# A hybrid decoder step on one NeuronCore: attention values by head and a later normalisation, tiles zeroed once, and a tail in which decays move to ScalarE and loads to GpSimd's queue

## The chip, the cores and the metric

The kernel runs on one core of one Trainium2 chip. The metric is the time of one execution on the device, in microseconds. The core has five engines that run their own instruction streams in order and wait for one another by semaphores: TensorE (PE in the profile; PEld is its weight load), VectorE (DVE), ScalarE (ACT), GpSimd (POOL) and SyncE (SP). SP, ACT and POOL also issue DMAs.

## The reference, cut to what matters

One inference step of a decoder layer: 1024 prompt tokens and 32 sampled ones (8 sequences of 4), model width 1024, four head groups of width 512 that share one input and one output projection.

```python
# x <- LayerNorm(alpha * x + W_out [y_A | y_B | y_C | y_D])
# A: gated DeltaNet, 4 heads of 128, chunks of 64, solved in its triangular form
#    S_t = exp(g_t) S_{t-1} + beta_t k_t (v_t - exp(g_t) S_{t-1}^T k_t)^T,  o_t = S_t^T q_t
# B: Mamba-2 SSD, 8 heads of 64, 2 groups of B/C, state 64; gated by SiLU, then
#    y / rms(y) * w_norm
# C: FoX: softmax(q k^T + sum of log-forget gates, causal) v, 8 heads of 64, times a SiLU gate
# D: cross attention, 4 heads of 128, into 256 memory tokens
```

The step also attends the sampled tokens to 4096 cached ones per sequence, and returns the new caches and states.

## The kernel before

**Stages.** The trace falls into four stretches. From 0 to about 755 us the input projections run, mixed with the attention of the sampled tokens over the cached pages. From 755 to 1157 us FoX runs, woven with the DeltaNet solve and scan and with the rest of the projections. From 1157 to 1420 us is the tail: the output projection, mixed with the eight SSD chunks and the sampled tokens' last steps. The rest is the LayerNorm of the last token tile and its stores. All large products are in float32, split into a high and a low part where the projections need it.

**What sets the order.** The Python code issues steps of several generators in turn (`weave((fox, 64), (gdn, 37))`). A scheduler in the framework then reorders the instructions of each engine by its own planned times, and tile pools set the waits: a tile with `bufs=1` can be loaded again only when the last reader of its former content is done. A queue is never reordered on the chip: what stands behind a waiting instruction waits too.

**FoX** (`fox`). Four pairs of heads, one after the other. A pair loads `vt` (its values for all 1024 tokens, 512 KB, from the DRAM tensor `vD`, one buffer) and the gate `g2` on SP's queue, and q, k and the cumulative gates on GpSimd's. `with behind(self.gl, ...)` orders the SP loads behind a DeltaNet gate load. For each head: scores in PSUM tile `fs`, minimum and exponential on VectorE and ScalarE (`S`), transposes (`ft`) copied to `P`, products `fo<-P,vt` (L620), and VectorE multiplies `fo` into `g2`. After both heads the sums of the exponentials are inverted, spread over 64 columns (`rr`), transposed (`fr`), and multiplied into `g2` (L640).

**DeltaNet** (`gdn`). Eight units (four heads in two halves). `gdn_solve` inverts triangular blocks: it reads `A` (loaded on SP from the DRAM tensors `aD..A`, `big("A")`) and `D1`, whose diagonal 16x16 blocks come from the DRAM tensor `dX` by eight DMAs on SP (L1041) after VectorE has zeroed the tile (L1039). `gdn_scan` then carries the state over the chunks (`su` matmuls) and loads `qd`, `Kt`, `QK` and its gate `g2` (L1051).

**SSD** (`ssd`). Each of eight chunks loads `E` (printed as `bE`), `bx` and a gate on SP. GpSimd copies the C rows of `bx` into a zero-padded tile `Cz` (L1355), so that one matmul (`bb`) makes both groups' products. VectorE takes the difference of cumulative decays for each of 8 heads (L1378), ScalarE the exponential, GpSimd multiplies by `cb` (L1382). The result `y` goes, times the norm weight, to the DRAM tensor `mixD[1]`.

**Output projection** (`out`, `mixed`, `out_w`). 16 row blocks of `w_out` in four groups of four (12 to 15, 8 to 11, 0 to 3, then 4 to 7, SSD's group). For each group and each of eight token tiles `mixed` loads the mixer tile `mr` (256 KB, on SP), ScalarE makes the high part `mh`, GpSimd the rest `ml` (L1546), and 24 matmuls `op` of 128x512 follow (L1574). The tiles have two buffers. In the last group the sampled tokens' tile (8) stands first; its matmul reads `accs`, which VectorE adds up in `out_s` (L1535); after each tile comes its LayerNorm (`lr` and `acc` on GpSimd).

## Time and profile before

| | us |
|---|---|
| timed runs | 1434.15, 1447.03, 1447.47 (median 1447.03) |
| the profiled execution | 1434.86 |
| its span in the trace | 1433.1 |
| PE busy in the span | 1329.7 (93%) |
| DVE, ACT, POOL busy | 823.8, 494.7, 442.4 |

The span is what the trace covers; the profiled execution's own time is 1.8 us longer. In a row of the trace the number in brackets is the time for which the engine stood idle just before the instruction, and behind the arrow is what ended that idle time. Digits at the end of names are left out, so that `g` stands for the `g2` tiles and `D` for `D1`.

### The profile page before, as it was taken

The numbers are of one execution on the slowest core, as the hardware profiler recorded it, in microseconds if no ns is written. First come the engines' busy times: TensorE is split into PE (matmuls) and PEld (weight loads), VectorE is DVE, ScalarE is ACT, GpSimd is POOL, SyncE is SP. The second block draws the span as 40 slices with busy tenths as digits, with TensorE's granted clock in tenths as the row PEclk, the third lists the DMA queues.
The fourth block names the chain that finished last, engine by engine and source line by source line (L and its number), as shares of the span: only waits on it lengthen the run. The fifth ranks groups of instructions, "written<-read, shape, count | busy, mean of one in ns | idle before, by whom it ended". The sixth has DMA issues, their size and how long they took to land. (4 is left out here: it accounts for less than half of the span.)

```text
span 1433.1 us, 30270 instructions
## 1 busy us (share of the span) xinstructions
PE 1329.7 (93%) x11222; PEld 1110.0 (77%) x11222; DVE 823.8 (57%) x2141; ACT 494.7 (35%) x1280; POOL 442.4 (31%) x465
## 2 busy tenths in 40 slices
PE   7999999999899999999998899898988979999995
PEld 6899888888778877888887878776766756666764
DVE  4523223256576767534245655677676648856588
ACT  4422222233435343322233244454444421213232
POOL 1445322233425444432212100011111026544456
PEclk9999999999999999999999999899999999999998
DMA  6559888978778897888877834657547576655322
GB/s 246 196 169 374 331 299 323 321 269 281 240 284 306 282 307 248 303 287 323 308 259 175 239 91 118 239 147 208 137 129 252 175 234 205 198 160 121 96 67 106
DMA packets 184477, 324.30 MB, mean 226 GB/s; under 512 B 47177, under 2 KB 110954, under 8 KB 184330
## 3 DMA queue, kind: packets, MB, share of 16 engines
q1 hardware_dynamic: 113744, 241.39, 50.4%
q10 hardware_dynamic: 41930, 59.11, 11.6%
q0 software_dynamic: 28656, 21.88, 6.2%
q8 instruction: 88, 1.44, 0.4%
q14 instruction: 59, 0.48, 0.1%
HBM read 262.23 MB, written 60.01 MB: 225 GB/s over the span
## 5 line engine op out<-in xcount | busy, mean ns | idle before, releaser
L356 PE MATMUL pj<-xh,wh 128*128 128x352 f32 x1152 | 382.2, 333 | 13.1 <-ACT wh L341 5.0
L356 PE MATMUL pj<-xh,wl 128*128 128x352 f32 x1152 | 379.5, 329 | 3.3 <-DVE wl L342 3.3
L356 PE MATMUL pj<-xl,wh 128*128 128x352 f32 x1152 | 379.1, 329 | 0.0
L356 PEld LDWEIGHTS pj<-xh,wh 128*128 128x128 f32 x1152 | 219.1, 191 | 28.1 <-issue 10.7
L356 PEld LDWEIGHTS pj<-xh,wl 128*128 128x128 f32 x1152 | 219.8, 191 | 11.5 <-issue 6.3
L356 PEld LDWEIGHTS pj<-xl,wh 128*128 128x128 f32 x1152 | 219.3, 190 | 10.6 <-issue 9.9
L1574 PE MATMUL op<-wo,mh 128*128 128x512 f32 x512 | 162.9, 398 | 3.1 <-DVE lr L1587 1.6
L672 POOL DMA_INDIRECT lf<-in_logf,ix x64 | 67.9, 1062 | 203.4 <-DVE cb L675 163.4
L342 POOL TENSOR_TENSOR wl<-wr,wh 128x1024 fp32r<-128x1024 f32 x41 | 97.9, 2387 | 104.3 <-ACT wh L341 94.3
L742 DVE SCALAR_TENSOR_TENSOR Oacc<-Oacc,dmb,dO 128x512 f32<-128x512 f32 x64 | 47.5, 743 | 142.3 <-PE dO L737 134.1
L1574 PEld LDWEIGHTS op<-wo,mh 128*128 128x128 f32 x512 | 95.6, 190 | 29.6 <-issue 6.0
L1574 PE MATMUL op<-wo,ml 128*128 128x512 f32 x256 | 102.0, 401 | 5.5 <-POOL ml L1546 5.5
L917 DVE SCALAR_TENSOR_TENSOR y<-u,cw,y 128x1080 f32<-128x1080 f32 x54 | 80.1, 1484 | 21.9 <-ACT y L915 21.5
L718 PEld LDWEIGHTS dA<-pg,QD 128*32 128x32 f32 x2048 | 59.8, 109 | 39.7 <-issue 25.8
L718 PE MATMUL dA<-pg,QD 128*32 128x128 f32 x2048 | 80.6, 275 | 7.6 <-DMA pg<-in_cache 7.5
L598 ACT ACTIVATE S<-S,mn 128x512 f32<-128x512 f32 (+2 forms) x96 | 58.5, 610 | 50.8 <-DVE mn L592 24.3
L737 PE MATMUL dO<-pg,dP 128*32 128x512 f32 x512 | 71.8, 605 | 4.1 <-ACT dP L734 3.9
L726 ACT ACTIVATE dmb<-dmb 128x1 f32<-128x1 f32 x64 | 18.7, 293 | 131.6 <-DVE dmb L725 116.3
L1574 PEld LDWEIGHTS op<-wo,ml 128*128 128x128 f32 x256 | 48.4, 189 | 20.2 <-POOL ml L1546 7.1
L592 DVE CUSTOM_DVE_ANT_0 S<-fs,cB 128x512 f32<-128x512 f32 (+2 forms) x96 | 52.5, 551 | 19.9 <-PE ft L219 15.0
L1193 POOL TENSOR_TENSOR rb<-ra,constG 128x4 f32<-128x4 f32 (+1 forms) x9 | 8.7, 971 | 156.5 <-DVE ra L1192 156.5
L620 PE MATMUL fo<-P,vt 128*64 128x128 f32 x576 | 47.9, 288 | 9.6 <-DMA vt<-vD 7.7
(521 smaller groups left out, 2450.2 us busy)
## 6 DMA issues: line engine op xcount, KB each, us to landing
pg<-in_cache SPq DMA_DIRECT2D x256, 512.0 KB
wr<-in_w_in SPq DMA_DIRECT2D x48, 512.0 KB
k<-kD POOLq DMA_DIRECT2D x16, 512.0 KB, 18.2
wq<-in_w_out SPq DMA_DIRECT2D x16, 512.0 KB
mr<-mixD SPq DMA_DIRECT2D x32, 256.0 KB
xr<-in_xT SPq DMA_DIRECT2D x8, 528.0 KB
gateD<-gt ACTq DMA_DIRECT2D x24, 176.0 KB
mrow<-in_w_mem SPq DMA_DIRECT2D x8, 512.0 KB
```

What stands on the lines that cost most here:

```text
L342: (eng or self.se).tensor_tensor(out=l, in0=r, in1=h.bitcast(F32), op=ALU.subtract)
L356: nc.tensor.matmul(ps[:n], lhsT=w[:, k, :], rhs=x[:, k, s], start=(k == 0 and q == 0), stop=(k == KD - 1 and q == 2))
L592: nc.vector.tensor_tensor_reduce(out=S[:, :w], in0=p[:, :w], in1=cB[:, c0:c1], op0=ALU.add, op1=ALU.min, scale=1.0, scalar=3e38, accum_out ...
L598: nc.scalar.activation(out=S[:, :w], in_=S[:, :w], func=AF.Exp, scale=-1.0, bias=mn[:, 0:1], accum_out=rs[:, qt, h2, i:i + 1])
L620: d = nc.tensor.matmul(o[64 * half:64 * half + 64, 0:128], lhsT=vt[:, kt, 64 * h2:64 * h2 + 64], rhs=P[qt, b4], start=(kt == 0), stop=(kt ...
L672: nc.gpsimd.indirect_dma_start(out=lf, out_offset=None, in_=I["logf"], in_offset=bass.IndirectOffsetOnAxis(ap=ix[:, j:j + 1].bitcast(U32), ...
L718: nc.tensor.matmul(ps[32 * b:32 * b + 32, 0:n], lhsT=QD[:, 4 * gr + b, hp, :], rhs=key(hp, b), start=(hp == 0), stop=(hp == 3), tile_posit ...
L726: nc.scalar.activation(out=mb[:, 1:2], in_=m, func=AF.Exp, scale=-1.0, bias=mb[:, 0:1])
L737: nc.tensor.matmul(po[32 * b:32 * b + 32, :], lhsT=P[:n, 32 * b:32 * b + 32], rhs=value(b), start=True, stop=True, tile_position=(0, 32 * b))
L742: nc.vector.scalar_tensor_tensor(out=O_, in0=O_, scalar=mb[:, 1:2], in1=po, op0=ALU.mult, op1=ALU.add)
L917: nc.vector.scalar_tensor_tensor(out=y, in0=u[:, i:i + CWD], scalar=w[:, i:i + 1], in1=y, op0=ALU.mult, op1=ALU.add)
L1574: nc.tensor.matmul(p[:m], lhsT=l[:, k, :], rhs=W[k][0][:, w, s], start=(k == 0 and q == 0), stop=(k == kn - 1 and q == 2))
```

## The change

FoX: `vt` is held by head (256 KB) with two buffers, and the load of each head is issued at the head's start; the projection writes `vD` in that layout. The normalisation becomes a generator, `fox_norm`, that runs in two steps within the next pair's work, and for the last pair at the end. DeltaNet: two lasting tiles `D1z` are zeroed once by GpSimd in place of a `D1` zeroed by VectorE for each unit; the second content of `D1` gets a tile of its own. SSD: `Cz` and its copies go; two matmuls over 64 rows each, into two PSUM tiles, make the products. The eight differences of a chunk go from VectorE to ScalarE (Relu, then Exp with scale -1). The multiplication by the norm weight goes from `y` into `w_out`'s rows 4 to 7. Output: the weights of the next group are loaded one group ahead into a second pool, mixer tiles have three buffers and are loaded by GpSimd's queue (all but the first two), and the last group takes the sampled tokens' tile second.

```diff
 def fox_v(self, hp):
+        vv = vt[:, :T].rearrange("p (h n c) -> p n h c", h=2, c=64)
-            self.copy(vt[:, 512 * a:512 * a + 512], p)
+            self.copy(vv[:, 4 * a:4 * a + 4], p.rearrange("p (n h c) -> p n h c", h=2, c=64))
-    def fox(self, hp):
+    def fox(self, hp, ended):
-        vt = fx.tile([128, 8, 128], F32, tag="vt", name="vt", bufs=1)
...
-            if h2 == 0:
-                with behind(self.gl, hd - GL):
-                    nc.sync.dma_start(vt, self.vD[hp].rearrange("p (n c) -> p n c", c=128))
+            vt = fx.tile([128, 8, 64], F32, tag="vt", name="vt", bufs=2)
+            with behind(self.gl, hd - GL):
+                nc.sync.dma_start(vt, self.vD[hp][:, 512 * h2:512 * h2 + 512].rearrange("p (n c) -> p n c", c=64))
+                if h2 == 0:
                     nc.sync.dma_start(g2, self.gateD[8 + hp])
...
+                next(ended, None)
                 o = self.g("fo")
...
+        return self.fox_norm(hp, g2, rs)
+
+    def fox_norm(self, hp, g2, rs):
         ri = fx.tile([128, 8, 2], F32, tag="ri", name="ri", bufs=2)
...
+            if a == 1:
+                nc.scalar.dma_start(self.mixD[2][:, hp, :], g2)
+            yield
 def gdn(self):
+        self.D1z = [self.ga.tile([128, 4, 32], F32, name=f"D1z{i}") for i in range(2)]
+        for t in self.D1z:
+            nc.gpsimd.memset(t, 0.0)
 def gdn_inv(self, i):
-        D1 = self.ga.tile([128, N, 32], F32, tag="D1", name="D1", bufs=2)
-        nc.vector.memset(D1, 0.0)
+        D1 = self.D1z[i % 2]
 def ssd(self):
-            for g in range(2):
-                nc.gpsimd.tensor_copy(cz[G[g], g, :], bx[G[g], 5, :])
...
-            nc.tensor.matmul(p[:, 128:384], lhsT=bx[:, 4, :], rhs=cz, start=True, stop=True)
+            p2 = self.g("bb")
+            for g, o in enumerate((p[:, 128:256], p2[:, 0:128])):
+                nc.tensor.matmul(o, lhsT=bx[G[g], 4, :], rhs=bx[G[g], 5, :], start=True, stop=True)
...
             for hh in range(8):
-                nc.vector.tensor_scalar(out=E[:, hh, :], in0=E[:, hh, :], scalar1=self.gam[:, n, 4 + hh:5 + hh], scalar2=0.0,
-                                        op0=ALU.subtract, op1=ALU.min)
-            nc.scalar.activation(out=E, in_=E, func=AF.Exp)
+                nc.scalar.activation(out=E[:, hh, :], in_=E[:, hh, :], func=AF.Relu, scale=-1.0, bias=self.gam[:, n, 4 + hh:5 + hh])
+            nc.scalar.activation(out=E, in_=E, func=AF.Exp, scale=-1.0)
...
-            nc.vector.tensor_tensor(out=y, in0=y, in1=_bc(self.pv[:, 91:95], 128), op=ALU.mult)
 def out_w(self, k0, k1, pool=None):
+            if k0 == 4:
+                f = self.pv[:, 87 + k:88 + k]
+                nc.scalar.activation(out=w[:, 0, :], in_=r, func=AF.Identity, scale=f)
+                nc.vector.scalar_tensor_tensor(out=w[:, 1, :], in0=r, scalar=f, in1=w[:, 0, :].bitcast(F32), op0=ALU.mult, op1=ALU.subtract)
 def mixed(self, k0, k1, n):
-        raw, mh, ml = (self.ow.tile([128, kn, 128], d, tag=t, name=t, bufs=2) ...
-        nc.sync.dma_start(raw, self.mixD[k0 // 4][:, q0:q0 + kn, n * 128:(n + 1) * 128])
+        pool, nb, eng = self.mixp                    # (ow, 2, nc.sync) at first, then (op, 3, nc.gpsimd)
+        raw, mh, ml = (pool.tile([128, kn, 128], d, tag=t, name=t, bufs=nb) ...
+        eng.dma_start(raw, self.mixD[k0 // 4][:, q0:q0 + kn, n * 128:(n + 1) * 128])
 def out(...):
-        for n in ((8,) if last else ()) + tuple(range(8)):
+        for n in (0, 8, 1, 2, 3, 4, 5, 6, 7) if last else range(8):
 the calls in the tail, with KO = (8, 0):
+                V = self.out_w(KO[0], KO[0] + 4, ow2)
                 run(self.out(12, 16, W, first=True, pre=pre))
-                for k in KO:
-                    W = self.out_w(k, k + 4)
-                    self.out_s(k, W)
-                    run(self.out(k, k + 4, W))
+                self.out_s(KO[0], V)
+                W = self.out_w(KO[1], KO[1] + 4)
+                run(self.out(KO[0], KO[0] + 4, V))
```

TensorE's instructions stand in the same order in both programs up to the one that runs at about 755 us in the trace of before, so the first of the four stretches is the same.

On SP's queue, at the load of the third pair's values (`vt<-vD_81`) in the program before (`g_12226` is the DeltaNet's second gate tile, `D_12851` a `D1` tile, `dq` and `g_15416` belong to cross attention):

```order
L1057 DMA Kp<-aD2Kp 128x512
L809 DMA dq<-dqD_86 128x1024
L1051 DMA g_12226<-gateD_125 128x512
L568 DMA vt<-vD_81 128x1024
L1041 DMA D_12851<-dX_122 16x4x16 x5
L1057 DMA A<-aD2A 128x512
L1041 DMA D_12851<-dX_122 16x4x16 x3
```

The same place in the changed program, where one pair has two such loads:

```order
L1064 DMA g_12226<-gateD_125 128x512
L570 DMA vt<-vD_81 128x512
L1054 DMA D1z_11226<-dX_122 16x4x16 x8
L1070 DMA A<-aD2A 128x512
L819 DMA dq<-dqD_86 128x1024
L1070 DMA Vp<-aD2Vp 128x512
L1070 DMA Kp<-aD2Kp 128x512
L1070 DMA Kt<-aD2Kt 128x512
L1070 DMA qd<-aD2qd 128x512
L1070 DMA QK<-aD2QK 128x512
L821 DMA g_15420<-gateD_134 128x1024
L1064 DMA g_12620<-gateD_126 128x512
```

The pair's first load still stands behind the DeltaNet's gate; a DeltaNet unit's loads and the next gate, `g_12620`, stand between it and the second head's, which follows two rows later. Counted in `fo` matmuls on TensorE's queue (288 in all), the eight DeltaNet units' last steps stand behind 72, 108, 137, 161, 190, 216, 245 and 281 of them before, and behind 39, 72, 101, 129, 154, 183, 216 and 245 now.

On TensorE, at the end of FoX's second pair in the program before (`fr` is the normalisation, `cT` cross attention, `lp`, `lt` and `su` DeltaNet):

```order
L620 MATMUL fo<-P,vt 64x128 x7
L219 MATMUL fr<-constG,rr 128x128 x4
L219 MATMUL cT<-constG,P 128x128 x3
L588 MATMUL fs<-k_13209,q_13208 128x512
L589 MATMUL fs<-k_13210,q_13208 128x512
L591 LDWEIGHTS identb
L591 MATMUL fs<-foxm,identb 128x128
L1092 MATMUL lt<-P_12482,D_12089 32x16 x16
L1164 MATMUL su<-u,Kt 128x128
L1165 MATMUL su<-u,QK 128x128
L1167 MATMUL su<-S,qd 128x128
L219 MATMUL fr<-constG,rr 128x128 x4
```

And the end of a pair in the changed program:

```order
L624 MATMUL fo<-P,vt 64x128 x7
L219 MATMUL fr<-constG,rr 128x128 x4
L591 MATMUL fs<-k_13187,q_13186 128x512
L592 MATMUL fs<-k_13188,q_13186 128x512
L1173 MATMUL su<-S,wkT 128x128
L1119 MATMUL lp<-DT_12845,A 32x32 x8
L219 MATMUL cT<-constG,P 128x128 x4
L219 MATMUL ft<-constG,S 128x128 x3
```

The second `fr` now follows three `fo` later, with the next pair's work and more of the DeltaNet's between the two.

On GpSimd's queue, around one SSD chunk in the program before (`hst` and `Cg` belong to the chunk ahead, `rsB`, `xtl` and `bE` follow):

```order
L1405 TENSOR_TENSOR hst<-hst,hcd 128x256
L1376 TENSOR_TENSOR Cg<-Cg,bx 128x512
L1355 COPY Cz_16195<-bx 64x128 x2
L1546 TENSOR_TENSOR ml<-mr,mh 128x512 x2
L1416 TENSOR_TENSOR rsB<-bso,constG 128x1
L1362 TENSOR_TENSOR xtl<-xdt,etl 128x512
L1382 TENSOR_TENSOR bE<-bE,cb 128x512 x2
L1546 TENSOR_TENSOR ml<-mr,mh 128x512
```

And in the changed program:

```order
L1414 TENSOR_TENSOR hst<-hst,hcd 128x256
L1386 TENSOR_TENSOR Cg<-Cg,bx 128x512
L1560 TENSOR_TENSOR ml<-mr,mh 128x512
L1558 DMA mr<-mixD_136 128x4x128
L1560 TENSOR_TENSOR ml<-mr,mh 128x512
L1558 DMA mr<-mixD_136 128x4x128
L1425 TENSOR_TENSOR rsB<-bso,constG 128x1
L1369 TENSOR_TENSOR xtl<-xdt,etl 128x512
L1391 TENSOR_TENSOR bE<-bE,cb 128x512
L1560 TENSOR_TENSOR ml<-mr,mh 128x512
L1391 TENSOR_TENSOR bE<-bE,cb 128x512
L1558 DMA mr<-mixD_136 128x4x128
```

The copies `Cz`, ahead of two `ml`, are gone, and each `ml` has a load beside it. In the last group seven of the eight loads stand ahead of the first LayerNorm step on this queue.

## Rows read from the trace of the kernel before

**Rows 1.** Stretches: length; busy (xcount) of PE, PEld, DVE, ACT, POOL; PEclk, DMA, GB/s.

```profile
0.00:755.00 755.00, 720.13 (x6247) 634.16 (x6248) 370.29 (x937) 253.53 (x661) 259.90 (x274) 0.99 0.81 283
755.00:1157.00 402.00, 363.05 (x3567) 295.73 (x3569) 264.08 (x819) 173.26 (x516) 46.52 (x66) 0.95 0.59 175
1157.00:1420.00 263.00, 246.18 (x1414) 180.06 (x1406) 180.15 (x373) 66.42 (x101) 130.01 (x120) 0.99 0.50 147
1141.00:1157.00 16.00, 11.99 (x127) 8.73 (x131) 11.91 (x47) 5.44 (x17) 2.75 (x7) 1.00 0.59 200
```

**Rows 2.** PE's order of time, FoX stage: start, us, instruction, [idle before <-releaser].

```profile
1004.17 0.69 PE L620 MATMUL fo<-P,vt 128*64 128x128 f32 x4 [7.71 <-DMA vt<-vD]
...
1089.90 0.47 PE L219 MATMUL fr<-constG,rr 128*128 128x128 f32 x1 [5.02 <-DVE g L640]
```

**Rows 3.** The stretches just behind three stalls; PEclk is the granted clock.

```profile
1004.00:1009.00 5.00, 4.83 (x18) 3.98 (x19) 2.14 (x5) 0.44 (x2) 0.00 (x0) 0.50 0.00 0
1090.00:1095.00 5.00, 5.00 (x23) 4.71 (x24) 4.67 (x13) 2.62 (x6) 2.48 (x3) 0.53 1.00 365
1303.00:1307.00 4.00, 4.00 (x11) 3.19 (x12) 0.00 (x0) 0.00 (x0) 4.00 (x5) 0.59 0.44 131
```

**Rows 4.** SP's queue in order of time, third pair's loads.

```profile
992.60 0.32 SPq L1051 DMA_DIRECT2D g<-gateD  x1
993.01 0.41 SPq L568 DMA_DIRECT2D vt<-vD  x1
```

**Rows 5.** DVE in order of time, two units of DeltaNet.

```profile
898.51 0.28 DVE L1082 TENSOR_TENSOR AL<-A,constG 32x128 f32<-32x128 f32 x1 [7.40 <-DMA A<-aD1A]
...
1086.25 0.28 DVE L1082 TENSOR_TENSOR AL<-A,constG 32x128 f32<-32x128 f32 x1 [4.07 <-DMA A<-aD3A]
```

**Rows 6.** What SP's queue waited for: total us, times, longest.

```profile
SPq L1041 <- DVE D L1039: 45.9, 4, 16.5
```

**Rows 7.** PE's order of time, tail.

```profile
1246.69 0.50 PE L1574 MATMUL op<-wo,ml 128*128 128x512 f32 x1 [1.81 <-POOL ml L1546]
...
1277.90 0.50 PE L1574 MATMUL op<-wo,ml 128*128 128x512 f32 x1 [0.95 <-POOL ml L1546]
...
1302.81 0.77 PE L1574 MATMUL op<-wo,ml 128*128 128x512 f32 x1 [2.78 <-POOL ml L1546]
...
1372.12 0.62 PE L1576 MATMUL op<-accs,constG 128*32 128x512 f32 x1 [2.79 <-DVE accs L1535]
```

**Rows 8.** POOL in order of time, one SSD chunk's start in the tail.

```profile
1300.78 0.63 POOL L1355 COPY Cz<-bx 64x128 f32<-64x128 f32 x2 [9.18 <-DMA bx<-bD]
1301.49 1.26 POOL L1546 TENSOR_TENSOR ml<-mr,mh 128x512 fp32r<-128x512 f32 x1
```

**Rows 9.** Groups by line and shape from 1157 us, xcount | busy, mean.

```profile
L1546 POOL TENSOR_TENSOR ml<-mr,mh 128x512 fp32r<-128x512 f32 x30 | 40.7, 1358 | 41.1 <-ACT mh L1545 40.6
L1602 POOL TENSOR_TENSOR acc<-acc,lb 128x512 f32<-128x512 f32 x14 | 19.4, 1392 | 10.8 <-DVE acc L1601 5.6 <-DVE lr L1587 5.2
L1378 DVE TENSOR_SCALAR bE<-bE,gam 128x128 f32<-128x128 f32 x64 | 18.1, 344 | 10.2 <-DMA bE<-gS 5.4 <-ACT Cg L1375 4.9
L1588 POOL TENSOR_TENSOR lr<-lr,constG 128x1 f32<-128x1 f32 x8 | 4.8, 601 | 0.0
L1545 ACT CAST mh<-mr 128x512 fp32r<-128x512 f32 x30 | 18.5, 617 | 75.0 <-PE op L1574 52.2 <-DMA mr<-mixD 12.8 <-issue 5.4
L1367 ACT COPY bt<-bb 128x128 f32<-128x128 f32 x8 | 2.1, 263 | 14.5 <-PE bb L1365 14.5
```

**Rows 10.** The tile op alone in a stretch of the last group.

```profile
1374.00:1418.00 44.00, 42.38 (x184) 34.07 (x184) 11.29 (x16) 0.00 (x0) 1.00 0.25 86
```

**Rows 11.** POOL in order of time: two of its DMA issues.

```profile
767.01 0.59 POOL L1057 DMA_DIRECT2D A<-aD0A  x1 [0.30 <-POOL bs L923]
771.03 0.86 POOL L561 DMA_DIRECT2D q<-qD  x1
```

**Rows 12.** The page's costliest groups: POOL's indirect DMAs.

```profile
L672 POOL DMA_INDIRECT lf<-in_logf,ix x64 | 67.9, 1062 | 203.4 <-DVE cb L675 163.4
```

More of the change, by code (lines that the diff above doesn't have):

```diff
@@ L1079, in gdn_solve @@
             self.gdn_inv(i + 1)
[L1080 removed]
+        nc.vector.transpose(out=fl(DT1), in_=fl(D0))
         for q in Q:
@@ L1339, in ssd @@
             nc.gpsimd.tensor_copy(cd[G[g]], self.cdP[G[g], :, 4 + 4 * g:8 + 4 * g])
-        Cz = [sb.tile([128, 2, 128], F32, name=f"Cz{i}") for i in range(2)]
-        for c in Cz:
-            nc.gpsimd.memset(c, 0.0)
         gam8 = self.gS.rearrange("(c n) t -> n c t", n=8)
@@ L1693, in foxes @@
             def foxes():
+                ended = iter(())
                 for hp in range(4):
-                    yield from self.fox(hp)
+                    ended = yield from self.fox(hp, ended)
+                run(ended)
             fox, gdn = foxes(), self.gdn()
```

40 lines of the change are left out of this document (22 added, 18 removed).

## The prediction

> **What bounds the kernel now.** I read the stretches first. Up to 755 us TensorE is busy for 720 of 755 us, from there to 1157 us for 363 of 402, and in the tail for 246 of 263 [rows 1]. No other engine comes near: in the tail GpSimd has 130 us and VectorE 180 of 263, in FoX's stretch VectorE has 264 of 402 [rows 1]. So TensorE bounds every stretch, and a change is worth what it takes out of TensorE's idle time, 39 us in FoX's stretch and 17 us in the tail, plus what the clock loses behind a stall. The reader is to look at TensorE's order of time next, at the instruction that ended each long stall, and then on the engine named there, at what it had waited for.
>
> In FoX's stretch two stalls stand out that the change touches: 7.71 us at 1004.17, ended by the DMA that brought a pair's values, and 5.02 us at 1089.90, ended by VectorE's `g` in the normalisation [rows 2]. In the tail I take four: 1.81, 0.95 and 2.78 us ended by GpSimd's `ml`, and 2.79 us ended by `accs` [rows 7]. Behind three of these TensorE ran for 4 to 5 us at a granted clock of 0.50, 0.53 and 0.59 [rows 3], that is at or near the lower of its two levels, 1.2 GHz, though it was busy all the time. Taken against full clock this costs 5 x 0.50 = 2.5, 5 x 0.47 = 2.3 and 4 x 0.41 = 1.6 us. Shorter stalls get no such term.
>
> **The values by head.** In the program before, the pair's 512 KB go out at 993.01, directly behind a DeltaNet gate load at 992.60 on SP [rows 4], and TensorE stands until 1004.17. In the changed program there are two buffers of one head each, so the next pair's first load needs only the former pair's first head to be done, half a pair earlier, and half the bytes. The gate load still stands ahead of it on the queue, and would hold it as before if the DeltaNet were as late as before; but the DeltaNet's last steps stand 29 to 36 `fo` matmuls earlier, about half a pair of 72. So I take the whole stall: -7.7 - 2.5 = **-10.2**. What is late next at that place is the minimum and the exponential, which both programs have there.
>
> **The normalisation within the next pair.** The stall of 5.02 us is one of a chain: the second `fr` needs VectorE's product with the first, and VectorE stood for 4.07 us until `A` of the DeltaNet had come, at 1086.25, 3.7 us before TensorE went on [rows 5]. Moving `fr` behind three `fo` of the next pair gives TensorE work between the two, but VectorE still stops when `A` is late, and everything that TensorE does there passes VectorE. Bounds: 0, if the wait ends elsewhere, and -5.0 - 2.3 = -7.3. I take **-3**, nearer to nothing, because VectorE's wait is not touched by this part.
>
> **The tiles zeroed once.** SP waited 45.9 us in four waits, once 16.5 us, to start the loads into `D1` until VectorE had zeroed it [rows 6], and `A` is queued behind these loads. The eight zeroings go, and SP then waits only for the last reader of the tile two units before. That makes `A` earlier; VectorE's waits for it were 7.40 and 4.07 us [rows 5], which reach TensorE in part. Bounds 0 and -4.1 (the second whole); I take **-2**.
>
> **The DeltaNet's earlier end.** The order moves the DeltaNet ahead, and its last unit ends behind 245 of 288 `fo`, before behind 281. The last 43 `fo` then run with less to fill TensorE's gaps. A measure of such a stretch is the last 16 us of the stage before, with TensorE busy for 11.99, or idle for 25% [rows 1], against 10% in the whole stretch. 43 of 288 is 15% of 402 us, 60 us, of which about half is FoX's own work (an estimate): 30 us x 15% = 4.5. Bounds 0, if the cross attention fills it, and 9 with all 60 us; I take **+4**. This is the price of the first part: the same shift that frees the gate load takes filler from the end. FoX's stretch together: -10.2 - 3 - 2 + 4 = **-11**.
>
> **The copies in the tail.** All three `ml` stalls have one cause, seen on GpSimd: the copy into `Cz` of the next chunk waits 9.18 us for the DMA that brings `bx`, and the `ml` that TensorE needs stands right behind it in the queue [rows 8]. With the copies gone the `ml` stand behind `Cg`, which reads the chunk's own data. -1.81 - 0.95 - 2.78 - 1.6 = **-7.1**. The products move to two matmuls of half the columns, so TensorE's work stays. The first instruction on GpSimd that now needs the new `bx` is `xtl`; ahead of it stand one or two `ml` more, so that I expect its wait to hide. Bounds 0 to -7.1 belong to a rival below.
>
> **The last group's order.** The sampled tokens' matmul stands second, so `accs` has a token tile's time more, 24 x 44 / 184 = 5.7 us at the last group's pace [rows 10], against 2.79 us of stall: **-2.8**.
>
> **Loads on GpSimd's queue.** 30 loads take GpSimd's own time. Nearby issues of plain DMAs took 0.59 and 0.86 us there [rows 11], an indirect one 1.06 [rows 12]: 30 x 0.59 to 1.06 = 18 to 32 us on an engine that has 133 us to spare in the tail. In the last group GpSimd has per token tile `ml` 1.36, `lr` 0.60 and twice `acc` 1.39, 4.7 us [rows 9], and TensorE needs 5.7 us, so 1.0 us is left, a little more than a plain issue. But seven of the eight loads stand ahead of the first LayerNorm step, with three buffers behind them. Bounds 0 and 7 x 1.06 = +7.4, if they all delay the chain; I take **+1**. A gain I exclude: none of the stalls in [rows 7] was ended by such a load.
>
> **What I cost at nothing.** The eight differences per chunk take 0.344 us each off VectorE [rows 9]. On ScalarE the nearest row of that size is the copy of 128x128 at 0.263 us [rows 9]: 64 x 0.26 = 17 us on an engine busy for 66 of 263. They come ahead of an `mh` of 0.62 us [rows 9] by 8 x 0.26 = 2.1 us at most, covered by a token tile's 5.7 us of matmuls; without that cover 8 chunks x 2.1 = 17 us. The norm weight in `w_out`, the earlier weights and the four buffers for sampled states take away waits that ended no stall of [rows 7]. The drain behind the last matmul keeps its order.
>
> **The sum.** FoX -11.2; tail -7.1 - 2.8 + 1 = -8.9; together -20.1, which makes 1434.9 - 20.1 = 1414.8 against the profiled execution. The median of the three runs is 1447.0, 12.2 us above it, and two of three runs lie there, so at the median's level the same sum gives 1426.9. I predict **1420**, between the two. With all ends at their best: -10.2 - 7.3 - 4.1 - 7.1 - 2.8 = -31.5, 1403. At their worst: -10.2 + 9 - 7.1 - 2.8 + 7.4 = -3.7, 1431 at the profiled level and 1443 at the median's.
>
> **Rivals.**
> First, the stalls in FoX only move: VectorE stops for `A` as before, the values come in time but the next pair's first `fo` waits for VectorE instead, and the end of the stretch has no filler. For it speaks that the stretch has VectorE busy for 264 of 402 us and that its waits are untouched by two of three parts; against it, that the longest stall was a plain transfer. FoX's stretch then gives 0, the tail -8.9: 1426 against 1434.9, within 1%.
> Second, slower: the mixer tiles come late because their loads stand in GpSimd's queue. A load is issued three tiles ahead at best, two tiles of cover are 11.5 us; less `mh` and `ml`, 2.0 us together, 9.5 us are left for a wait on the queue, the issue and the transfer. A wait as that of `Cz`, 9.18 us [rows 8], now on `xtl`, uses this up, and from there each tile behind a chunk is late. Price: at each of 8 chunks the stall at 1302.81 with its clock, 2.78 + 1.6 = 4.4, so +35; with FoX at -11 and `accs` at -2.8 the sum is 1456. For it: `xtl` needs the same transfer, and loads stand behind it in every chunk. Against: it stands later in the chunk than `Cz` did.
> The nearest rows for an issue are 0.59 to 1.06 us while VectorE was at work too. The Trainium skill, SBUF — State Buffer, section "SBUF: two separate sides", speaks against this part: it says that GpSimd cannot write the descriptors of its own DMAs while VectorE runs an operation in a two-port mode, and gives about 620 ns alone and 3100 ns then. By it 30 x 3.1 = 93 us, an estimate from that page, would fill most of GpSimd's idle time in the tail; no row here shows an issue that long.
> Third, the change doesn't do what it says: the values still come behind a late gate load, since that load stands ahead of them on SP in both programs, and GpSimd's wait for `bx` moves to `xtl` with the `ml` behind it. Then only `accs` is gained: 1432.
>
> **Chances.** The forecast 0.58: the causes of the two largest terms are each seen on the engine that waited. The first rival 0.22, the third 0.10, the second 0.10. A measurement of this kernel can tell about 1%, 14 us, from no change. The forecast lies beyond that, the first and the third rival within it, the second on the other side: faster 0.58, same 0.32, slower 0.10. The range takes the forecast's ends at both levels, **1403 to 1443**; the first rival lies in it (1426, at the median's level 1438), the third at the profiled level; what is left out is the second and part of the third.
>
> **What would show it.** In the changed kernel's trace the stall ended by `vt` should be gone and none over 3 us stand ahead of a pair's first `fo`; SP's wait for VectorE's zeroing should be gone and VectorE's waits for `A` shorter; `ml` should end no stall over 1 us behind a chunk's start, and GpSimd's loads should take 0.5 to 1.1 us each. From the first pair's end to the last `fo` the stretch should be some 11 us shorter, the tail some 9. I am wrong if TensorE's idle time near the last pair grows by more than 9 us, or if GpSimd waits at `xtl` as it did at `Cz`.

## The result, and the profile after

The changed kernel takes 1480.39 us (median of 4 runs) against 1442.28 for the kernel before, measured beside it; the ratio is 1.0273, with a 95% interval of 1.021 to 1.0336. I had forecast 1420 with a range up to 1443. The profiled execution has a span of 1476.5 us against 1433.1.

The windows of the changed kernel, cut at the last `dO` of the decode, the last `fr` of FoX and the last `op` (columns as in [rows 1]):

```profile
770.80:1185.60 414.80, 355.81 (x3398) 290.16 (x3391) 250.56 (x787) 166.42 (x500) 47.07 (x63) 0.93 0.59 165
1185.60:1461.60 276.00, 261.66 (x1439) 189.24 (x1437) 162.99 (x304) 85.46 (x165) 142.38 (x130) 0.94 0.45 139
1461.60:1476.50 14.90, 0.40 (x2) 0.00 (x0) 10.82 (x18) 1.72 (x3) 6.51 (x6) 0.67 0.28 106
```

The same cuts in the kernel before (770.0, 1155.6, 1419.9):

```profile
770.00:1155.60 385.60, 348.88 (x3394) 284.54 (x3387) 254.12 (x792) 167.05 (x500) 45.35 (x62) 0.95 0.60 176
1155.60:1419.90 264.30, 247.48 (x1425) 180.63 (x1424) 181.16 (x377) 66.42 (x101) 129.91 (x120) 0.99 0.50 146
1419.90:1433.10 13.20, 0.42 (x2) 0.00 (x0) 9.34 (x13) 1.52 (x2) 6.04 (x6) 0.59 0.32 119
```

The first 770 us are the same within 0.8 us. FoX's stretch is 414.8 us long against 385.6, +29.2; the tail 276.0 against 264.3, +11.7; the drain 14.9 against 13.2. Each length can be taken apart: TensorE's idle time is the length less its busy time, and the clock's part is the length times one less PEclk (rounded to 0.01 in the row, so to 2 us here). In FoX's stretch idle time went from 36.7 to 59.0 us and the clock's part from 19 to 29; in the tail idle time fell from 16.8 to 14.3 and the clock's part rose from 3 to 17. What is left, TensorE's work at full clock, is the same within 3 us. The clock's part counts a low clock also while TensorE stands, where it costs nothing, so the two overlap a little. So FoX's stretch lost some three quarters by standing (22.3 of 29.2 us) and the rest by the clock behind it, and the whole loss of the tail is clock.

The long stalls of TensorE in the changed kernel's order of time:

```profile
937.27 0.47 PE L219 MATMUL ft<-constG,S 128*128 128x128 f32 x1 [6.26 <-ACT P L214]
...
1077.19 0.58 PE L1177 MATMUL su<-u,Kt 128*128 128x128 f32 x1 [5.78 <-DVE u L1174]
...
1113.64 0.47 PE L219 MATMUL ft<-constG,S 128*128 128x128 f32 x1 [11.96 <-ACT P L214]
...
1201.76 0.48 PE L219 MATMUL bt<-constG,bx 128*128 128x128 f32 x1 [4.01 <-DMA bx<-bD]
...
1287.59 0.33 PE L1398 MATMUL by<-bE,xdt 128*64 128x128 f32 x2 [2.45 <-POOL bE L1391]
...
1295.59 0.80 PE L1588 MATMUL op<-wo,mh 128*128 128x512 f32 x1 [3.22 <-ACT wo L1529]
...
1310.99 0.48 PE L1398 MATMUL by<-bE,xdt 128*64 128x128 f32 x2 [3.16 <-POOL bE L1391]
```

None of the stalls of [rows 2] and [rows 7] is there: no `fo` waits for `vt`, no `op` for `ml`, and `accs` ends none. Others stand in their place, longer ones. In the tail one is a wait of TensorE itself for `bx`, the load that `Cz` had waited for before [rows 8]. What had the engines named in FoX's stretch waited for? The rows of ScalarE, VectorE and SP behind the stalls at 937, 1077 and 1113 us:

```profile
936.36 0.34 ACTq L1190 DMA_DIRECT2D out_pgs<-S  x1
936.74 0.48 ACT L214 COPY P<-ft 128x384 f32<-128x384 f32 x1 [6.69 <-DMA mk<-mkD]
...
1074.45 0.28 DVE L1095 TENSOR_TENSOR AL<-A,constG 32x128 f32<-32x128 f32 x1 [7.38 <-DMA A<-aD3A]
...
1097.94 0.60 SPq L1558 DMA_DIRECT2D mr<-mixD  x1
...
1112.36 0.62 ACT L1559 CAST mh<-mr 128x512 fp32r<-128x512 f32 x1 [11.68 <-DMA mr<-mixD]
...
1113.00 0.58 ACT L214 COPY P<-ft 128x512 f32<-128x512 f32 x1
```

At 1113 ScalarE's copy of `P`, which FoX's `fo` needs, stood in its queue behind `mh`, the conversion of the output projection's first mixer tile; its load was issued on SP at 1097.94 and came 14 us later. At 1077 VectorE stood 7.38 us for the `A` of a DeltaNet unit, where the waits of [rows 5] were 7.40 and 4.07 us, and the scan of an earlier unit, which TensorE needed next, stood behind it. At 937 ScalarE stood 6.69 us and copied `P` only when it had issued a store of a DeltaNet state, `out_pgs<-S`. Each time an instruction at the head of an engine's queue waits for a load, or to issue a store, and work of another stage or unit stands behind it.

### The profile page after: what moved, and what is told of

It reads as the page before. It is cut to its first block, busy times and chain, and to the rows that moved or that the text cites. A ratio compares the mean times of both kernels' runs of the same rounds, so it can differ in the third digit from the quotient of the medians.

```text
span 1476.5 us, 30258 instructions
## 1 busy us (share of the span) xinstructions
PE 1348.6 (91%) x11238; PEld 1122.6 (76%) x11238; DVE 806.3 (55%) x2069; ACT 513.5 (35%) x1344; POOL 458.0 (31%) x479
## 3 DMA queue, kind: packets, MB, share of 16 engines
q10 hardware_dynamic: 41930, 59.11, 11.4%
## 5 line engine op out<-in xcount | busy, mean ns | idle before, releaser
L356 PE MATMUL pj<-xh,wh 128*128 128x352 f32 x1152 | 383.2, 333 | 15.4 <-ACT u L214 8.6
L1588 PE MATMUL op<-wo,mh 128*128 128x512 f32 x512 | 168.2, 409 | 3.2 <-ACT wo L1529 3.2
L565 POOL DMA_DIRECT2D k<-kD x16 | 13.2, 828 | 186.8 <-PE fs L594 153.5
L219 PE MATMUL ft<-constG,S 128*128 128x128 f32 x288 | 50.1, 292 | 22.1 <-ACT P L214 19.3
L1560 POOL TENSOR_TENSOR ml<-mr,mh 128x512 fp32r<-128x512 f32 x32 | 43.4, 1358 | 77.9 <-ACT mh L1559 77.8
L736 ACT ACTIVATE dmb<-dmb 128x1 f32<-128x1 f32 x64 | 18.8, 293 | 130.2 <-DVE dmb L735 125.1
```

Of the source, the lines that this page charges most:

```text
L219: self.nc.tensor.transpose(out, in_, self.c("ident", n)[:, :n])
L356: nc.tensor.matmul(ps[:n], lhsT=w[:, k, :], rhs=x[:, k, s], start=(k == 0 and q == 0), stop=(k == KD - 1 and q == 2))
L1560: nc.gpsimd.tensor_tensor(out=ml, in0=raw, in1=mh.bitcast(F32), op=ALU.subtract)
L1588: nc.tensor.matmul(p[:m], lhsT=l[:, k, :], rhs=W[k][0][:, w, s], start=(k == 0 and q == 0), stop=(k == kn - 1 and q == 2))
```

## The experiments

Each run gives its median, and its ratio to the kernel before, run on the same chip. The lengths of FoX's stretch (from the last `dO` to the last `fr`) and of the tail (from there to the last `op`) are from the profiled executions, one for each kernel. They vary by themselves: a stall of TensorE near 800 us, ended by VectorE's `wl` of the last projections, takes 1.1 us in the kernel before, 7.8 in e3, 8.2 in t4 and 9.3 in t9, with the same order of instructions there, so that differences of up to some 8 us between FoX lengths are read with it:

| kernel | median us | ratio (95%) | FoX us | tail us |
|---|---|---|---|---|
| before | 1436 to 1442 | 1 | 385.6 | 264.3 |
| after | 1480.39 | 1.0273 (1.021 to 1.0336) | 414.8 | 276.0 |
| e1_fox | 1478.57 | 1.0277 (1.0222 to 1.0332) | 414.6 | 282.9 |
| e2_tail | 1464.87 | 1.0177 (1.0116 to 1.0239) | 388.2 | 286.2 |
| e3_vt | 1442.17 | 1.0043 (1.001 to 1.0077) | 387.3 | 267.9 |
| e5_d1z | 1481.16 | 1.031 (1.0254 to 1.0365) | 414.0 | 278.9 |
| v1_d1z_dve | 1442.75 | 1.0026 (0.9984 to 1.0068) | 385.7 | 262.6 |
| v3_poolms0 | 1470.28 | 1.0215 (1.0161 to 1.0268) | 412.3 | 271.3 |
| v4_d1z_nopre | 1475.12 | 1.0259 (1.0213 to 1.0305) | 412.8 | 280.1 |
| x1_fox_dve | 1448.88 | 1.0111 (1.0035 to 1.0187) | 378.2 | 279.6 |
| x2_after_dve | 1458.25 | 1.0152 (1.0071 to 1.0232) | 385.0 | 285.8 |
| t1_cz | 1450.94 | 1.0087 (1.0047 to 1.0127) | 385.6 | 277.0 |
| t2_norelu | 1464.31 | 1.0217 (1.0124 to 1.031) | 385.3 | 290.2 |
| t3_nomix | 1459.32 | 1.0184 (1.0093 to 1.0274) | 383.8 | 281.2 |
| t7_ahead | 1458.17 | 1.0128 (1.0087 to 1.0169) | 385.5 | 290.6 |
| t4_noahead | 1447.43 | 1.006 (1.0032 to 1.0088) | 391.0 | 272.3 |
| t9_cz_shs | 1454.24 | 1.0094 (1.0056 to 1.0131) | 395.3 | 275.3 |
| x6_fold_order | 1436.83 | 0.9991 (0.9956 to 1.0025) | 386.5 | 260.2 |
| y2_fox_relu | 1437.12 | 1.0003 (0.9968 to 1.0038) | 380.4 | 275.6 |
| y3_fox_mix | 1444.97 | 1.007 (1.0033 to 1.0108) | 382.5 | 271.9 |

### First round: which part

The theory that these rows suggest: FoX's stretch loses by the order, in which the DeltaNet stands ahead; the tail by ScalarE, which has the Relus and two groups of weights to convert. The rivals: the values by head or the normalisation, and GpSimd's loads.

**e1_fox**: the diff's changes in `fox_v`, `fox`, `fox_norm`, `gdn`, `gdn_inv` and `gdn_solve` alone.

> Values by head, normalisation within the next pair and tiles zeroed once, with the tail of before. In the changed kernel FoX's stretch ends 30 us later than before and the tail is 11 us longer. Theory: the two stretches are independent, so this kernel is +27 to +33 us against before. Rival: the tail's loss is a consequence of what FoX's stretch leaves behind (late stores, a low clock); then this kernel loses more than 36 us.

It lost 40 us by the ratio. FoX's stretch is that of the changed kernel (414.6 us), but the tail, with the code of before, is 18.6 us longer: the rival.

**e2_tail**: all the rest of the diff alone.

> The parts of the tail alone (no Cz, Relu, weight folded, weights ahead, tile order, mixer tiles by GpSimd), FoX's stretch of before. Theory: +8 to +14 us, since GpSimd's loads are not what is late, but ScalarE, which has the Relus and two groups of weights to convert. Rival: alone it gains the 9 us that I forecast, and loses only behind the later end of FoX's stretch.

It lost 25 us by the ratio, nearly all in the tail: more than expected. e1 and e2 together give more than the changed kernel's loss, so the two do not add; why, is left open.

**e3_vt**: values by head alone.

```diff
-        vt = fx.tile([128, 8, 128], F32, tag="vt", name="vt", bufs=1)
+            vt = fx.tile([128, 8, 64], F32, tag="vt", name="vt", bufs=2)
```

> Values by head alone. Theory: the stall of 7.7 us with its clock goes and nothing else moves much: -6 to -10 us. Rival: the later loads of the second head and the changed order cost what the stall gave, -2 to +6 us.

The rival's number holds: 0.4% slower. FoX's stretch is 1.7 us longer, or 5 us shorter if its longer stall of `wl` (7.76 for 1.13 us) is taken off. Its longest stall, with VectorE and SP ahead of it:

```profile
973.07 0.55 SPq L568 DMA_DIRECT2D vt<-vD  x1
...
981.72 0.86 SPq L1058 DMA_DIRECT2D A<-aD2A  x1
...
993.68 0.28 DVE L1083 TENSOR_TENSOR AL<-A,constG 32x128 f32<-32x128 f32 x1 [8.25 <-DMA A<-aD2A]
...
995.63 0.48 PE L621 MATMUL fo<-P,vt 128*64 128x128 f32 x2 [7.48 <-DVE P L216]
```

The load of the same `A` in the kernel before:

```profile
969.52 0.34 SPq L1057 DMA_DIRECT2D A<-aD2A  x1
```

The values are there in time: the third pair's first `fo`, behind 144 of the 288, which stood for 7.71 us before [rows 2], does not wait. But TensorE stands for 7.48 us in the second pair, behind 129 `fo`. There `P` is late, because VectorE, ahead of that copy, waited 8.25 us for `A` of the DeltaNet. That load now goes out behind the values; before, it went out 23 us ahead of them [rows 4], and VectorE did not wait for it. One stall has gone, and another of the same size has come with the new order of loads on SP's queue, which the rival had named.

**e5_d1z**: the tiles zeroed once alone.

```diff
+        self.D1z = [self.ga.tile([128, 4, 32], F32, name=f"D1z{i}") for i in range(2)]
+        for t in self.D1z:
+            nc.gpsimd.memset(t, 0.0)
...
-        nc.vector.memset(D1, 0.0)
+        D1 = self.D1z[i % 2]
```

> The two tiles zeroed once by GpSimd alone. Its order puts the DeltaNet's units ahead of FoX as in the changed kernel (last step behind 245 of 288 fo, before behind 281), the other FoX parts alone don't. Theory: this order is the loss in FoX's stretch, +20 to +32 us, with VectorE and ScalarE standing at loads that come late. Rival: taking the zeroing off SP's waits gains 2 to 4 us, and the loss belongs to the values by head or to the normalisation.

It has the whole loss of the changed kernel by itself, 45 us, 28 of it in FoX's stretch, where TensorE is idle for 56.6 us and the clock's part is 33 us:

```profile
772.40:1186.40 414.00, 357.45 (x3396) 290.62 (x3389) 251.84 (x786) 165.98 (x500) 45.43 (x62) 0.92 0.58 164
1186.40:1465.30 278.90, 256.26 (x1423) 187.38 (x1422) 181.06 (x370) 66.66 (x101) 132.59 (x120) 0.95 0.46 138
```

Its two longest stalls, with ScalarE ahead of each and VectorE's product into `g`:

```profile
933.93 0.68 DVE L640 TENSOR_TENSOR g<-fr,g 128x512 f32<-128x512 f32 x1
...
944.21 0.33 ACTq L641 DMA_DIRECT2D mixD<-g  x1
...
944.58 0.21 ACT L1089 COPY P<-lp 128x64 f32<-128x64 f32 x1 [10.34 <-DMA QK<-aD1QK]
...
944.85 0.36 PE L1094 MATMUL lt<-P,D1z 32*32 32x16 f32 x12 [8.99 <-ACT P L1089]
...
1121.98 0.62 ACT L1547 CAST mh<-mr 128x512 fp32r<-128x512 f32 x1 [13.54 <-DMA mr<-mixD]
...
1123.42 0.58 PE L1141 MATMUL wv<-Vp,DT 128*128 128x128 f32 x1 [10.91 <-ACT DT L1132]
```

The second is the wait for `mh` again, 13.54 us. In the first ScalarE stood for 10.34 us and went on when it had issued its store of a pair's result, `mixD<-g`, at 944.21, though VectorE's last product into that `g` began at 933.93. The profile names a DMA as what ended it.

### Second round: the tiles or the order

**v1_d1z_dve** and **v3_poolms0** each change which engine zeroes. In v1 it is the lasting tiles, in v3 the kernel before with one instruction on another engine:

```diff
 v1, against e5_d1z:
-            nc.gpsimd.memset(t, 0.0)
+            nc.vector.memset(t, 0.0)
 v3, against before:
-        nc.vector.memset(D1, 0.0)
+        (nc.vector if i else nc.gpsimd).memset(D1, 0.0)
```

> The lasting tiles as in the change, but zeroed once by VectorE; the order then has the DeltaNet's last steps behind 72, 101, ... 281 fo, as before. Theory: the loss of 45 us comes from the DeltaNet being put ahead of FoX, not from the tiles: within 8 us of before. Rival: the lasting tiles themselves cost (loads released by another reader, D1 in a tile of its own): over +25 us.

> The kernel before with one instruction moved: the first unit's D1 is zeroed by GpSimd, all other units as before. Its order has the DeltaNet's last steps behind 46, 75, ... 255 fo. Theory: this alone brings most of the loss, +20 to +45 us. Rival: the order is not what costs; then it is within 8 us of before, or gains the early start of the first unit.

Both went as the theory says: 1.0026 and 1.0215. FoX's stretch in v1 and in v3:

```profile
774.00:1159.70 385.70, 350.08 (x3395) 285.69 (x3388) 253.16 (x786) 167.50 (x500) 44.01 (x60) 0.95 0.61 176
```

```profile
769.50:1181.80 412.30, 359.71 (x3403) 291.35 (x3396) 252.86 (x798) 167.86 (x500) 45.58 (x62) 0.93 0.59 165
```

v3 removes nothing and keeps the `D1` tiles; it lets the first DeltaNet unit start without VectorE, and its stretch is 26.7 us longer (8.60 us of it is one stall at 835.33, behind a late weight of the projections, which may have another cause). In the kernel before VectorE comes to its first zeroing at 807 us, behind work for the decode. Without that edge the scheduler's order has the DeltaNet ahead; the first `lp` of the DeltaNet runs at 826 us and the first `fo` of FoX at 850, where in the kernel before they run at 844 and 827. The two have changed places.

**v4_d1z_nopre**: as e5, without the early mixer tiles.

```diff
-            pre = [self.mixed(12, 16, n) for n in range(2)]
+            pre = []
```

> The tiles zeroed once by GpSimd, and the two mixer tiles that are loaded and converted within FoX's stretch (mh on ScalarE, waiting for a load) loaded in the tail instead. Theory: ScalarE's wait of 13.5 us for mr and TensorE's 10.9 us behind it go: 10 to 15 us less than with the tiles alone, +30 to +35 us. Rival: the wait only passes to the next late load; then +40 to +48 us.

Only 6 us less than e5 by the medians, and FoX's stretch is as long (412.8 us): the rival, mostly. TensorE's longest stall in the place where it had stood for `mh`:

```profile
1120.18 0.65 PE L866 MATMUL zs<-cmk,QM 128*32 128x256 f32 x4 [6.22 <-DMA cmk<-in_cmk]
```

With `mh` out of the way TensorE stands for cross attention's cached keys, 6.22 us. So the wait for `mh` alone is not the cause of the 28 us; the order of the queues is: v1 changes one engine name in e5, the order with it, and the loss is gone. That the DeltaNet stands ahead is the difference that I see in all kernels with the loss; no run changes its place by other means.

**t1_cz**: no `Cz`, and the sampled tokens' tile second.

```diff
-            nc.tensor.matmul(p[:, 128:384], lhsT=bx[:, 4, :], rhs=cz, start=True, stop=True)
+            for g, o in enumerate((p[:, 128:256], p2[:, 0:128])):
+                nc.tensor.matmul(o, lhsT=bx[G[g], 4, :], rhs=bx[G[g], 5, :], start=True, stop=True)
```

> In the tail only: no Cz and the sampled tokens' tile second. Theory (my forecast for these terms): the ml stalls and the accs stall go, -6 to -12 us. Rival: the wait for bx passes to the next instruction that needs it on GpSimd or TensorE, -3 to +10 us.

0.9% slower, though no `op` waits for `ml` or `accs` any more. TensorE's two longest stalls in its tail, and the clock behind the second:

```profile
1184.78 0.59 PE L1570 MATMUL op<-wo,mh 128*128 128x512 f32 x1 [4.73 <-DVE acc L1576]
...
1281.64 0.69 PE L1474 MATMUL yi<-shs,sCM 128*64 128x256 f32 x1 [4.31 <-DMA shs<-in_sst]
```

```profile
1278.00:1298.00 20.00, 16.36 (x53) 10.59 (x54) 7.37 (x17) 1.61 (x4) 5.93 (x6) 0.66 0.33 103
```

A sampled state's load ended 4.31 us, and 20 us at a mean of 0.66 cost 6.8 us more. TensorE's idle time in the tail is 15.4 us, hardly less than the 16.8 of before. Some 9 us of its length are neither idle time nor clock (253 us of work against 244); the narrower products, 32 `bb` matmuls for 16, take 7.6 us busy against 4.8, and the rest I cannot place.

### Third round: with the order kept, and the tail's parts

**x1_fox_dve** and **x2_after_dve**: e1 and the changed kernel with v1's one line.

> All three FoX parts, but the lasting tiles zeroed by VectorE (one engine name), tail of before. The DeltaNet's last steps stand behind 72 to 281 fo, as before. Theory: the loss goes with the order, and the stalls that the parts remove come back as waits of VectorE or ScalarE for another load at the same place: -6 to +8 us against before, 35 us less than with GpSimd's zeroing. Rival: with the order kept the parts bring the 11 us of my forecast.

> The changed kernel with the same one engine name changed. Theory: FoX's stretch gives back its 29 us; the tail is then as with the tail's parts alone, +22 us against before, so +15 to +28 us in all. Rival: in the changed kernel the two losses are not separable, and it stays above +33 us.

x2 falls from 1480.39 to 1458.25, and its stretch of FoX is 385.0 us: this one engine name is what costs the changed kernel in FoX's stretch. Its tail is 9.8 us longer than the changed kernel's, so that 22 us come back and not 30. x1's windows:

```profile
771.40:1149.60 378.20, 351.81 (x3390) 285.16 (x3383) 251.57 (x776) 166.30 (x497) 43.74 (x60) 0.95 0.62 178
1149.60:1429.20 279.60, 261.62 (x1430) 188.06 (x1428) 185.06 (x387) 67.59 (x104) 129.78 (x121) 0.93 0.45 141
```

FoX's stretch is 7.4 us shorter than before, idle 26.4 us for 36.7: with the order kept the parts do bring most of the 11 us that I forecast for them. What has gone is the values' stall: no `fo` waits for `vt`, and none of the waits near it is over 2 us. The normalisation's has stayed, at the next pair's `ft`, behind a wait of VectorE for `A` of 3.99 us (4.07 before [rows 5]):

```profile
1086.27 0.47 PE L219 MATMUL ft<-constG,S 128*128 128x128 f32 x1 [5.89 <-DVE g L646]
```

But the tail, in which no line differs, is 15.3 us longer, nearly all clock (0.93 for 0.99), so that x1 is slower than before by the ratio. One stall there and the stretches behind it:

```profile
1208.20 0.33 PE L1399 MATMUL by<-bE,xdt 128*64 128x128 f32 x2 [1.90 <-POOL bE L1392]
```

```profile
1208.00:1212.00 4.00, 3.80 (x23) 2.31 (x24) 2.09 (x4) 0.00 (x0) 4.00 (x5) 0.59 0.14 55
1212.00:1216.00 4.00, 4.00 (x10) 1.19 (x9) 1.00 (x3) 0.00 (x0) 0.35 (x1) 0.50 0.79 262
1216.00:1220.00 4.00, 4.00 (x15) 1.87 (x14) 2.16 (x5) 1.26 (x2) 1.25 (x2) 0.50 0.28 74
1220.00:1224.00 4.00, 4.00 (x12) 2.62 (x10) 3.57 (x11) 1.69 (x2) 0.64 (x1) 0.70 0.37 107
1224.00:1228.00 4.00, 4.00 (x14) 2.22 (x14) 2.71 (x5) 0.25 (x1) 0.57 (x2) 1.00 0.76 236
```

TensorE is busy from the stall on, and yet it takes 14 us until it is at 2.4 GHz again: 1.90 us of waiting and 6.8 us of clock (4 x 0.41 + 4 x 0.5 + 4 x 0.5 + 4 x 0.3). In [rows 3] a stall of 2.78 us cost 1.6. What ran there differs: in x1 the first 10 us are `by`, `xsu` and `bh`, narrower than `op`, with two `op` among them; behind the stall of [rows 3] it is `op` alone. Whether this is the reason no run shows.

**t2_norelu** and **t3_nomix**: e2 without the Relu, and e2 without the mixer tiles' move.

```diff
 t2, against e2:
-                nc.scalar.activation(out=E[:, hh, :], in_=E[:, hh, :], func=AF.Relu, scale=-1.0, bias=self.gam[:, n, 4 + hh:5 + hh])
+                nc.vector.tensor_scalar(out=E[:, hh, :], in0=E[:, hh, :], scalar1=self.gam[:, n, 4 + hh:5 + hh], scalar2=0.0,
+                                        op0=ALU.subtract, op1=ALU.min)
 t3, against e2:
-        eng.dma_start(raw, self.mixD[k0 // 4][:, q0:q0 + kn, n * 128:(n + 1) * 128])
+        nc.sync.dma_start(raw, self.mixD[k0 // 4][:, q0:q0 + kn, n * 128:(n + 1) * 128])
```

> The tail's parts without the Relu: VectorE takes the eight differences again. With the Relu the tail's parts were +25 us. Theory: ScalarE's queue makes the exponentials and so GpSimd's bE late (stalls of 3.4, 2.3 and 1.0 us on TensorE, and the low clock behind them): +12 to +20 us. Rival: ScalarE is not what is late: +22 to +28 us.

> The tail's parts without the mixer tiles' move: two buffers, loads on SP. Theory: GpSimd's loads cost little by themselves, +20 to +28 us. Rival: loads in GpSimd's queue and the larger tiles (which shift what later tiles overlay in memory) are the cause, also of the 7.5 us for which GpSimd stood at the sampled tokens' memset: +5 to +15 us.

1464.31 and 1459.32 against 1464.87: neither is the cause, and the theory on ScalarE's Relu falls. The theory on GpSimd's loads, that they cost little, holds.

### Fourth round: the weights ahead

The orders show what e2, t2, t3 and the changed kernel share: on TensorE the sampled tokens' last SSD steps (`yy`, `yi`, `yu`, `yo`) stand at 181 to 192 `op` matmuls, ahead of the second group of 192. In the kernel before they stand between 192 and 292, with `op` matmuls between them.

**t7_ahead** and **t4_noahead**: the weights ahead alone, and e2 without them.

```diff
+                V = self.out_w(KO[0], KO[0] + 4, ow2)
                 run(self.out(12, 16, W, first=True, pre=pre))
-                for k in KO:
-                    W = self.out_w(k, k + 4)
-                    self.out_s(k, W)
+                self.out_s(KO[0], V)
+                W = self.out_w(KO[1], KO[1] + 4)
```

> The kernel before with the weights one group ahead and nothing else. Its order has all steps of the sampled tokens' SSD at 192 op matmuls, between the first and second group, before they stood between 173 and 292. Theory: they lose their filler, TensorE waits for each of their steps and runs at the low clock behind the waits: +12 to +25 us. Rival: weights that come earlier take no wait away and cost nothing: within 6 us.

> All of the tail's parts but the weights ahead; the sampled tokens' steps stand at 192 to 275 op matmuls, mixed with the second group. Theory: of the 25 us of the tail's parts 10 to 20 go, so +5 to +15 us. Rival: the loss is spread over the other parts: +20 to +26 us.

Loading weights earlier costs 22 us by the medians (1458.17 against 1436.37), and taking this out of e2 gives 17 back. The tail of t7, and from the sampled tokens' first step there to their last (`yy` to `yo`); the same steps in the kernel before; and three stalls of t7:

```profile
1157.00:1447.60 290.60, 263.79 (x1425) 192.53 (x1424) 183.74 (x377) 67.54 (x101) 122.75 (x120) 0.91 0.43 131
1245.80:1285.20 39.40, 27.99 (x174) 16.14 (x172) 24.85 (x60) 7.21 (x13) 13.92 (x18) 0.68 0.48 119
```

```profile
1236.60:1280.20 43.60, 39.56 (x230) 27.78 (x226) 30.88 (x58) 10.49 (x18) 18.51 (x17) 1.00 0.63 175
```

```profile
1271.83 0.37 PE L219 MATMUL ygs<-constG,gs 128*32 128x128 f32 x1 [2.99 <-DVE syt L1494]
...
1279.46 0.48 PE L1389 MATMUL by<-bE,xdt 128*64 128x128 f32 x2 [4.17 <-POOL bE L1382]
...
1304.94 0.80 PE L1574 MATMUL op<-wo,mh 128*128 128x512 f32 x1 [4.33 <-DVE acc L1580]
```

Idle 26.8 us, 10 more than before, and a clock's part of 26 us, 23 more. The short steps of the sampled tokens, and of the chunk that runs with them, wait for VectorE and GpSimd. Before, 100 `op` matmuls stood among the sampled tokens' steps, and TensorE was idle for 4.0 of 43.6 us at full clock; in t7 none does, and it is idle for 11.4 of 39.4 us at a mean of 0.68, 12.6 us of clock. So these steps have most of the idle time and over half of the clock; the rest lies ahead of them and behind.

**t9_cz_shs** and **x6_fold_order**: t1 with the norm weight folded and four buffers for sampled states, and the folded weight with the tile order alone.

```diff
 both:
-        for n in ((8,) if last else ()) + tuple(range(8)):
+        for n in (0, 8, 1, 2, 3, 4, 5, 6, 7) if last else range(8):
-            nc.vector.tensor_tensor(out=y, in0=y, in1=_bc(self.pv[:, 91:95], 128), op=ALU.mult)
 t9, with t1's matmuls:
-            hs = sb.tile([128, 2, 256], F32, tag="shs", name="shs", bufs=2)
+            hs = sb.tile([128, 2, 256], F32, tag="shs", name="shs", bufs=4)
```

> No Cz, the sampled tokens' tile second, the norm weight folded and four buffers for the sampled states. Without the last two it was +12 us, with a stall of 4.3 us for a sampled state and half clock behind it. Theory: that stall and its clock go, 8 to 11 us, so 0 to +5 us. Rival: the wait goes to the next step in the same place: +8 to +14 us.

> The sampled tokens' tile second in the last group and the norm weight folded into the weights; the order of all else on TensorE stays. Theory (a term of my forecast): the accs stall of 2.8 us goes, -2 to -4 us. Rival: something else is late at the last group's start, within 1 us of before or slower.

t9 loses as much as t1 (1.0094 for 1.0087), the rival again: no stall is ended by a state's load any more, but one of 4.8 us by GpSimd's `bE` and three of 2.1 to 2.3 us stand in the tail, which is 275.3 us long for 277.0. x6 keeps the order of everything else on TensorE; its tail is 260.2 us, 4.1 less than before, and no stall is ended by `accs`. In the timed runs it is the same as before, 0.9991 with 0.35% on either side, which does not rule out the 2 to 4 us expected.

**y2_fox_relu** and **y3_fox_mix**: x1's FoX with two other tails, in search of a kernel that beats both. Each is x1 with x6's two edits; y2 adds the Relu and the four buffers for sampled states, y3 the mixer tiles' move (`self.mixp = self.op, 3, nc.gpsimd`).

> All FoX parts with the tiles zeroed by VectorE; in the tail the Relu, the folded weight, the last group's order and four buffers for sampled states. Theory: FoX's stretch 378 us (8 less than before); the tail's loss hangs on where a stall falls, so the clock's part of it differs from the 18.8 us by over 5 us. Rival: the FoX parts leave the tail slower whatever stands there: 277 to 283 us of tail, clock's part 16 us and more.

> All FoX parts with the tiles zeroed by VectorE; in the tail the mixer tiles in three buffers by GpSimd's queue, the folded weight and the last group's order. Theory: as for the Relu, FoX's stretch 378 us, and the tail below 272 us, since the ml stalls and the accs stall go and no step of the sampled tokens is moved to a group's boundary. Rival: 277 us and more.

FoX's stretch keeps 5 and 3 us of its gain, the tails are 275.6 and 271.9 us. The clock's part, summed over stretches of 5 us, is 15.3 and 12.0 us against x1's 18.8 and 3.4 before: it changes with the order, by less than I expected in y2. Neither beats the kernel before (1.0003 and 1.007). I found no kernel that does by more than can be measured.

## Why the prediction was wrong, point by point

**What bounds the kernel** was read rightly: TensorE's work is the same within some 9 us in every stretch of every kernel, and the differences are for the most part idle time and clock. What failed is the next step, to price each part by itself, as if the order of all the rest stayed. The range had the same fault: its worst end, 1443, still holds the gains of the values and the copies whole.

**Values by head (-10.2).** The stall went in every kernel that has this part, and with the DeltaNet's order kept nothing of its size took its place (x1): so far the mechanism was right. Alone (e3) it brings at best -5 in FoX's stretch and nothing in the time, because the values' load now goes out ahead of `A`, and VectorE stands for `A` in the pair before. That is near my first rival, at 0.22, by an order of loads that I had not looked for; what I named as late next, the minimum and the exponential, it is not.

**Tiles zeroed once (-2) and the DeltaNet's earlier end (+4).** This is the step that failed. I saw in the order that the DeltaNet moves half a pair ahead, and counted it as a help for the values and as lost filler in the last 60 us, with +9 as the worst. It is +28 us (e5) and it lies all along the stretch. The +4 for the end was of the right size, as the last 60 us of FoX's stretch show, before and after: idle 4.6 and 8.9 us. So the sign of being wrong that I had set there, over 9 us more, stayed silent.

```profile
1095.60:1155.60 60.00, 55.45 (x674) 40.74 (x673) 40.53 (x158) 26.50 (x86) 5.13 (x10) 1.00 0.61 197
```

```profile
1125.60:1185.60 60.00, 51.14 (x531) 36.06 (x531) 39.39 (x150) 24.90 (x75) 5.43 (x9) 1.00 0.59 193
```

The loss stands ahead of it: the longest stalls lie from 937 to 1123 us in the changed kernel and in e5, where one stage's instructions at the head of ScalarE's and VectorE's queues wait for loads, or to issue a store, and hold the other stage. I priced the zeroing by SP's wait [rows 6], and took a wait removed for a gain. It is none: v1 takes SP's wait for the zeroing from 45.9 to 9.0 us, SP waits 26.6 us for the tile's last reader instead, and the stretch is as long as before. What cost was the engine of the first unit's zeroing (v3): in VectorE's queue it had kept the DeltaNet's first unit behind FoX's first pair, and the scheduler's order for everything after it hung on that.

**Normalisation within the next pair (-3).** No run has it alone. With the DeltaNet's order kept, all three FoX parts give -7.4 us in their stretch (x1; -5 and -3 in y2 and y3), where I had -15 for them without the filler's +4. The stall that this part was to shorten is still 5.89 us there, for 5.02 before, so it brought nothing: the bound of 0 that I gave, with the reason that I gave, VectorE's wait for `A`.

**The copies in the tail (-7.1).** The mechanism was right: no `op` waits for `ml` in the changed kernel or in t1. The gain is not there: t1 is 12 us slower (1450.94 against 1436.64), by a wait for a sampled state, its clock, and some 9 us of work that I could not place. The products, whose work I took to stay, have 7.6 us of TensorE's time for 4.8.

**The last group's order (-2.8)** is right in the profile of x6, with a tail 4.1 us shorter, and too small for its timed runs.

**Loads on GpSimd's queue (+1).** The issues took 0.75 to 0.83 us, median 0.79, all 30 of them, within the bounds from [rows 11, 12]. t3 shows no price beyond some us, so my slow-side rival named a wrong mechanism; in the changed kernel GpSimd stood for 1.6 us in all ahead of its eight `xtl`. The Trainium skill, SBUF — State Buffer, section "SBUF: two separate sides", gives about 3100 ns for such a load while VectorE runs an operation in a two-port mode; no issue here is that long, and no run shows whether VectorE was in that mode.

**What I cost at nothing.** The Relu took 0.387 us each, 25 us in all on ScalarE, and not 17; it cost nothing that t2 could show. The weights ahead are the wrong zero: 22 us (t7). I asked what waits they take away and found none; I did not ask the order what stands between the sampled tokens' steps once the second group may be placed otherwise.

**The clock.** I charged 1.6 to 2.5 us behind the three longest stalls and nothing behind shorter ones. In the tail the clock's part grew by more than the idle time: by some 16 us for 1 in x1, by 23 for 10 in t7.

Not settled: why x1's tail slows with the code of before (its order differs, since the scheduler places the tail behind another FoX), why e1's and e2's losses do not add and x2's tail is longer than the changed kernel's, and the 9 us of work in t1.
